# A four-layer decoder trunk on one core: joint key and value compression, a fixed first order, bias stores on ScalarE's queue, and a last sum by output halves

## The chip, the cores and the metric

The kernel runs on one core of one Trainium2 chip. The metric is the device time in microseconds (us) of one execution, and of several executions the median. TensorE (PE) multiplies matrices, VectorE (DVE) and ScalarE (ACT) work on elements, GpSimd (POOL) does little here, SyncE (SP) issues transfers (DMAs). Each engine takes its own instructions strictly in order.

## The reference

The input x has 256 rows of 1024 numbers. Four layers follow each other, each a feed-forward block, an attention and a second feed-forward block; all three normalise their input and their output:

```
x = x + 0.5 * rms_norm(swiglu(rms_norm(x, g[0]), ffn_w_in[i, 0], ffn_w_out[i, 0]), g[1])
hm = rms_norm(x, g[2])
m = sliding_sink_attention | nsa_attention | moba_attention   (layer i % 3)
x = x + rms_norm(m, g[3])
x = x + 0.5 * rms_norm(swiglu(rms_norm(x, g[4]), ffn_w_in[i, 1], ffn_w_out[i, 1]), g[5])
```

All attentions add a bias that depends on the distance of query and key, read from one table. Layer 1 (nsa_attention) also compresses keys and values: for each of the two, 15 overlapping blocks of 32 rows pass a two-layer perceptron:

```
flat = blocks.transpose(0, 1, 3, 2, 4).reshape(B, n_cmp, G, CMP_LEN * dh)
return jax.nn.gelu(flat @ w1) @ w2
```

## The kernel before, in words

The 256 rows are two chains (`Chain(0)`, `Chain(1)`) of 128 rows. Both use the same weights, which stream in once, as 625 pieces of 128x1024 f32 (512 KB, name `raw`, function `load`, four buffers). A piece is split (`feed`): ScalarE writes `hi`, its rounding to fp32r, and VectorE writes `lo`, the rest. x is transposed by TensorE (`split_T`, tile `trx`) and split likewise into `xh` and `xl`. A product is `hi·xh + lo·xh + hi·xl`: 12 matmuls of 512 columns for two pieces and one chain, in `proj` (into the tile `proj`) and in `accumulate` (into `acc`). Splits lie in a pool of 28 slots of 4 KB a partition (`k4`), which the attention stages share; `plan.want` keeps slots free for them.

Both chains are Python generators. A planner (`choose`) keeps a clock with estimated durations and takes, step by step, the chain that can go on earliest. TensorE's order is the order so written (`manual_schedule(engines=ORDERED)`); the order on the other engines, SyncE's DMAs among them, is set by a scheduler from the written order and its own estimates.

At the start, chain 0 transposes its x (x0), chain 1 its own (x1) some microseconds of the planner's clock later (`LATE`), and `first` squares x for the norm (`var`: two ScalarE squares into `junk`, two VectorE steps into `v`). `pres`, the norms' gains, is needed for `xh`.

`setup` starts after 30 steps. TensorE multiplies the table of biases with one-hot rows (tile `tab`), VectorE copies the rows, and four DMAs store them, each row repeated 32 times, in a scratch array in DRAM (`scratch<-k`, 384 KB each, 8 source partitions): table 1 in two halves of 8 heads, then table 0. They are issued by SyncE, in whose order all raws and bias loads stand, too. The attention of layer 0 reads table 1 back with shifted rows (`bias`, tile `bias`), four DMAs of 32 partitions for a group of heads.

In layer 1 `compress` runs first for keys (s = 0) and then for values (s = 1): 16 matmuls of 256 columns, written as 64x256, for each of four quarters of weights (`w1`, tile names `k<-w`) make the tile `hid` [64 partitions, 256]; a gelu of six instructions on 64 partitions, two transposes `hidT`, and the second layer `kcb` or `vcb` follow. (The hardware profile shows 32 matmul records for each of the two.) Beside it the attention's own steps run: `pv` products come in pairs whose results lie on the lower and upper 64 partitions.

At the end of each sublayer `accumulate` adds the last 12 products to the two halves (512 columns each) of `acc`, alternating between halves; `boundary` then squares both halves (`junk`), forms `r`, multiplies with the gain `g`, adds to x, and in the last layer sends x out.

Of the kernel before, what the change touches and what calls it, by code (L numbers as in the profile page):

```python
# [44 lines left out]
LATE = 6  # L45
SETUP = 30
SGAP = 8
# [5 lines left out]
ORDERED = {mybir.EngineType.PE}  # L53

# [196 lines left out]
class Engines:  # L251
    def __init__(self, nc, clock):
        self.tensor = TimedProducts(nc.tensor, clock)
        self.scalar = Timed(nc.scalar, "act", clock, 0.06, 0.00083)
        self.vector = Timed(nc.vector, "dve", clock, 0.065, 0.00105)
        self.gpsimd = Timed(nc.gpsimd, "pool", clock, 0.45, 0.001)
        self.sync = TimedLoads(nc.sync, clock)


@with_exitstack  # L260
def trunk(ctx: ExitStack, tc: tile.TileContext, x, rel, gains, pre, sinks, pos, w1, w2, wts, hot,
# [72 lines left out]
    def setup():  # L334
# [49 lines left out]
    def feed(urgent=False):  # L384

        load(plan.split + NRAW)
        if plan.split < len(halves) and (urgent or clock.now >= plan.at + PACE) and room() >= 2:
            i, half, n = halves[plan.split]
            r = raws.pop(plan.split)
            hi = p4.tile([P, HALF], F32R, tag="k4", name="hi")  # L390
            lo = p4.tile([P, HALF], F32R, tag="k4", name="lo")
            nc.scalar.activation(hi[:, :n], r[:, :n], AF.Copy)
            nc.vector.tensor_tensor(lo[:, :n], r[:, :n], hi[:, :n].bitcast(F32), op=ALU.subtract)
            parts.setdefault(i, []).append((hi, lo))
            ready_at[i] = max(when(lo) - 1.3 * half, ready_at.get(i, 0.0))
            plan.split += 1
            plan.at = max(plan.at + PACE, clock.now - 2.4)
            feed()
            return True
        return False  # L400

# [11 lines left out]
    class Chain:  # L413
# [36 lines left out]
        def split_T(self, src, q, norm=None):  # L450


            if q == 0:
                self.xh, self.xl = [], []
# [3 lines left out]
            ks = range(4 * q, 4 * q + 4)  # L458
            g = [None if norm is None else pres[:, norm, k:k + 1] for k in ks]
            for c, k in enumerate(ks):  # L460
                xh = px.tile([P, P], F32R, tag=f"xh{self.t}{k}", name="xh")
                if norm is None:
                    nc.scalar.activation(xh, p[:, c, :], AF.Copy)
                else:
                    nc.scalar.activation(xh, p[:, c, :], AF.Copy, scale=g[c])
                self.xh.append(xh)
            for c, k in enumerate(ks):
                xl = px.tile([P, P], F32R, tag=f"xl{self.t}{k}", name="xl")
                hi = self.xh[k].bitcast(F32)
                if norm is None:  # L470
                    nc.vector.tensor_tensor(xl, p[:, c, :], hi, op=ALU.subtract)
                else:
                    nc.vector.scalar_tensor_tensor(xl, p[:, c, :], g[c], hi, op0=ALU.mult,
                                                   op1=ALU.subtract)
                self.xl.append(xl)


        def first(self):
# [60 lines left out]
        def accumulate(self, acc, hh, hl, first, last):  # L539
# [4 lines left out]
            for n, (lhs, kk, part) in enumerate(terms):  # L544
                for nb in range(2):
                    nc.tensor.matmul(acc[nb], lhs[kk], got[kk][part][:, nb * 512:(nb + 1) * 512],
                                     start=first and n == 0, stop=last and n == 5)
# [340 lines left out]
        def attn_b(self, i):  # L888
# [22 lines left out]
            for s in range(2):  # L911
# [3 lines left out]
                if t == 0 and s == 0:  # L915
                    plan.want[3] = 3
# [29 lines left out]
    def compress():  # L946

        vbd = k4(2, [P, 2, 8, DH])
        nc.vector.memset(kcb, 0.0)
        hv = k2([P, 2, 2, 4, 32])  # L950
        for s in range(2):
# [4 lines left out]
            for e in range(2):  # L956
                rows = slice(DH * e, DH * e + DH)
                for m in range(2):
# [3 lines left out]
                        .broadcast_to([DH, 8, 4, NCMP]), op=ALU.add)  # L962
            drop(2)
            plan.want[2] -= 1
            ws = []
            for q in range(2):
                w = k4(3, [P, HALF])
                nc.sync.dma_start(w, w1[2 * s, :, q * HALF:(q + 1) * HALF])
                ws.append(w)
            p = bank([64, 2, P], "hid")  # L970
            for q in range(4):
                w = ws[q]
                yield when(w, xf), False
                for j in range(4 * q, 4 * q + 4):
                    at = (j % 4) * CMP_HIDDEN
                    nc.tensor.matmul(p.rearrange("p c n -> p (c n)"),
                                     xf[:, j].rearrange("p g n -> p (g n)"),
                                     w[:, at:at + CMP_HIDDEN], start=j == 0, stop=j == 15)
                drop(3)
                if q < 2:  # L980
                    w = k4(3, [P, HALF])
                    nc.sync.dma_start(w, w1[2 * s + 1, :, q * HALF:(q + 1) * HALF])
                    ws.append(w)
            drop(3)
            hid = k2([64, 2, P])
            q = k2([64, 2, P])
            nc.scalar.activation(q, p, AF.Square)
            nc.vector.tensor_scalar(q, q, 0.044715, 1.0, op0=ALU.mult, op1=ALU.add)
            nc.vector.tensor_tensor(q, q, p, op=ALU.mult)
            nc.scalar.activation(q, q, AF.Tanh, scale=GELU_C)  # L990
            nc.vector.tensor_scalar(q, q, 1.0, 0.5, op0=ALU.add, op1=ALU.mult)
            nc.vector.tensor_tensor(hid, q, p, op=ALU.mult)
            yield max(when(hid), free_bank()), False
            p = bank([P, 2, 64], "hidT")
            for c in range(2):
                nc.tensor.transpose(p[:, c, :], hid[:, c, :], ident[:64, :64])
            hid = k2([P, 2, 64])
# [112 lines left out]
```

## Time and profile before

| | us |
|---|---|
| median of three runs | 1984.88 |
| lowest, highest | 1984.06, 1987.67 |
| the profiled execution | 1989.9 |
| span of its instructions | 1988.1 |
| TensorE busy in it | 1947.6 |
| VectorE, ScalarE busy | 1236.2, 1040.7 |
| DMA, mean over the span | 179 GB/s |

The profiled execution is another execution than the three timed ones. Span is from its first instruction to its last; a little lies around it. Rows of the profile name the line of the helper that issues an operation (L228 a matmul, L235 a transpose, L210 a ScalarE or VectorE operation, L248 a DMA), so tiles, not lines, tell operations apart. A stretch's granted clock is TensorE's, 1.00 for 2.4 GHz throughout and 0.5 for 1.2 GHz throughout.

### The profile page before, as it was taken

How to read it: one execution, taken by the hardware profiler on the slowest of the kernel's cores; microseconds unless marked ns; L12 is line 12 of the kernel's file. 1: busy time of each engine (PE TensorE's matmuls, PEld its weight loads, DVE VectorE, ACT ScalarE, POOL GpSimd, SP SyncE). 2: the span in 40 equal slices, each digit the busy share in tenths (PEclk: the TensorE clock that was granted, in tenths of full speed). 3: DMA queues.
4: the chain of work that ended last, by engine and by line, in shares of the span. 5: the costliest groups of instructions: out<-in, count | busy, mean ns of one | idle time of the engine just before them, and what ended most of it. 6: DMA issues, size and time to landing. Idle time of an engine off the chain costs nothing. (4 is left out here: it accounts for less than half of the span.)

```text
span 1988.1 us, 27346 instructions
## 1 busy us (share of the span) xinstructions
PE 1947.6 (98%) x9948; PEld 1589.5 (80%) x9948; DVE 1236.2 (62%) x2271; ACT 1040.7 (52%) x1886; POOL 37.1 (2%) x62
## 2 busy tenths in 40 slices
PE   7999999999999999999999999999999999999998
PEld 6778878888888886788888887778888888878886
DVE  6556676556655648765566556466556655667553
ACT  6445665445544555554455446565445544665442
POOL 0000000000000000000000000000000000000000
PEclk9999999999999999999999999999999999999999
DMA  8578556555555454365555555556555555536551
GB/s 265 172 230 238 173 143 199 190 188 184 191 190 191 141 180 109 119 199 191 185 183 193 188 184 179 178 147 201 184 186 186 195 185 185 177 106 207 188 184 57
DMA packets 114099, 356.42 MB, mean 179 GB/s; under 512 B 12811, under 2 KB 30475, under 8 KB 113964
## 3 DMA queue, kind: packets, MB, share of 16 engines
q1 hardware_dynamic: 113964, 354.68, 55.3%
q8 instruction: 78, 1.28, 0.2%
q14 instruction: 57, 0.47, 0.1%
HBM read 352.01 MB, written 2.62 MB: 178 GB/s over the span
## 5 line engine op out<-in xcount | busy, mean ns | idle before, releaser
L210 DVE TENSOR_TENSOR lo<-raw,hi 128x1024 fp32r<-128x1024 f32 x625 | 761.0, 1223 | 378.0 <-ACT hi L210 346.9
L210 ACT ACTIVATE hi<-raw 128x1024 fp32r<-128x1024 f32 x625 | 660.6, 1064 | 383.4 <-PE acc L228 202.1
L228 PE MATMUL proj<-hi,xh 128*128 128x512 f32 (+1 forms) x1696 | 675.7, 400 | 2.6 <-DVE xl L210 1.9
L228 PE MATMUL proj<-lo,xh 128*128 128x512 f32 (+1 forms) x1696 | 658.7, 389 | 0.8 <-DVE lo L210 0.8
L228 PE MATMUL proj<-hi,xl 128*128 128x512 f32 (+1 forms) x1696 | 449.2, 387 | 0.0
L228 PEld LDWEIGHTS proj<-hi,xh 128*128 128x128 f32 x1696 | 320.6, 189 | 64.4 <-ACT xh L210 3.0
L228 PEld LDWEIGHTS proj<-lo,xh 128*128 128x128 f32 x1696 | 321.2, 189 | 61.5 <-DVE lo L210 1.1
L228 PEld LDWEIGHTS proj<-hi,xl 128*128 128x128 f32 x1696 | 316.2, 188 | 67.7
L228 PE MATMUL acc<-hi,hh 128*128 128x512 f32 x704 | 219.5, 393 | 3.0 <-ACT hh L210 3.0
L228 PE MATMUL acc<-lo,hh 128*128 128x512 f32 x704 | 217.7, 390 | 0.0
L228 PE MATMUL acc<-hi,hl 128*128 128x512 f32 x704 | 188.8, 390 | 0.0
L210 ACT ACTIVATE h<-proj,rh 128x256 f32<-128x256 f32 x176 | 82.0, 466 | 189.7 <-PE proj L228 189.6
L210 ACT ACTIVATE hh<-trh 128x256 fp32r<-128x256 f32 x176 | 66.9, 380 | 177.7 <-PE trh L235 177.6
L228 PEld LDWEIGHTS acc<-hi,hh 128*128 128x128 f32 x704 | 131.3, 189 | 30.1 <-ACT hh L210 3.7
L228 PEld LDWEIGHTS acc<-lo,hh 128*128 128x128 f32 x704 | 132.7, 189 | 27.9
L228 PEld LDWEIGHTS acc<-hi,hl 128*128 128x128 f32 x704 | 132.2, 188 | 27.7
L210 DVE SCALAR_TENSOR_TENSOR h<-h,proj 128x256 f32<-128x256 f32 x176 | 73.6, 418 | 120.0 <-ACT h L210 119.9
L210 DVE TENSOR_TENSOR hl<-trh,hh 128x256 fp32r<-128x256 f32 x176 | 73.9, 420 | 112.2 <-ACT hh L210 112.2
L210 ACT ACTIVATE k<-k,nm 128x128 f32<-128x128 f32 (+1 forms) x160 | 70.7, 446 | 35.8 <-DVE nm L210 35.7
L210 DVE SCALAR_TENSOR_TENSOR h<-proj,c,h 128x256 f32<-128x256 f32 x176 | 85.0, 483 | 5.2
L235 PE MATMUL trh<-ident,h 128*128 128x128 f32 x352 | 67.0, 272 | 0.0
L235 PEld LDWEIGHTS trh<-ident,h 128*128 128x128 f32 x352 | 48.7, 139 | 22.4 <-PE tab L228 0.6
(100 smaller groups left out, 1116.3 us busy)
## 6 DMA issues: line engine op xcount, KB each, us to landing
raw<-wts SPq DMA_DIRECT2D x624, 512.0 KB, 4.5
bias<-scratch SPq DMA_DIRECT2D x96, 128.0 KB, 5.0
g<-gains SPq DMA_DIRECT2D x12, 512.0 KB, 4.9
k<-w SPq DMA_DIRECT2D x8, 512.0 KB, 6.0
scratch<-k SPq DMA_DIRECT2D x4, 384.0 KB
out<-x SPq DMA_DIRECT2D x4, 256.0 KB, 2.1
x<-x SPq DMA_DIRECT2D x2, 256.0 KB
x<-x SPq DMA_DIRECT2D x1, 512.0 KB
```

Of the source, the lines that this page charges most:

```text
L210: return call(out, *args, **kw)
L228: self.engine.matmul(out, lhs, rhs, **kw)
L235: self.engine.transpose(out, src, ident)
```

## The change

Four things are changed.

- `compress` computes the hidden layer for keys and values together. The results of key branch and value branch lie on the lower and upper 64 partitions of one tile, written alternately; the sum over 16 positions is made in two parts of 8, each for its own four quarter loads; VectorE adds the parts. One gelu and one pair of transposes serve both. `plan.want[3]` keeps six slots instead of three.
- The start: `pres` is loaded first, by ScalarE's queue. Chain 0 alone begins. Its two transposed halves (`lift`) are followed by 16 transposes of the identity (`warm_up`); on ScalarE and VectorE the order of squares, splits of x and the first four splits of weights (`take`) is fixed. Chain 1 starts once chain 0 has taken its first weights, and its squares and splits come behind the third and fourth split.
- The four stores of the bias table are issued on ScalarE's queue.
- In the last `accumulate` of a sum, all six products of output half 0 come before the six of half 1.

```
+WARM = 16
-LATE = 6
+SPLITTERS = {mybir.EngineType.Activation, mybir.EngineType.DVE}
...
-                nc.sync.dma_start(scratch[i, h:h + 8],
-                                  rows[h:h + 8, i, :].unsqueeze(1).broadcast_to([8, REP, LT]))
+                nc.scalar_loads.dma_start(scratch[i, h:h + 8],
+                                          rows[h:h + 8, i, :].unsqueeze(1)
+                                          .broadcast_to([8, REP, LT]))
...
+    def warm_up():
+        p = bank([P, 4, P], "warm")
+        for n in range(WARM):
+            nc.tensor.transpose(p[:, n % 4, :], ident, ident)
...
             x_ = xt[self.t]
-            for q in range(2):
-                self.split_T(x_, q, 0)
-            self.v = self.var([x_[:, :512], x_[:, 512:]], 1.0)
+            if self.t == 0:
+                with tc.manual_schedule(engines=SPLITTERS):
+                    ps_ = [self.lift(x_, q) for q in range(2)]
+                    warm_up()
+                    self.v = self.var([x_[:, :512], x_[:, 512:]], 1.0)
+                    for q in range(2):
+                        self.split(ps_[q], range(4 * q, 4 * q + 4), 0)
+                        for _ in range(2):
+                            load(plan.split + NRAW)
+                            begun[:] = take()
+            else:
+                with tc.issue_after(begun[0].ins), tc.issue_after(begun[1].ins):
+                    for q in range(2):
+                        self.split_T(x_, q, 0)
+                    self.v = self.var([x_[:, :512], x_[:, 512:]], 1.0)
...
-            for n, (lhs, kk, part) in enumerate(terms):
-                for nb in range(2):
...
+            steps = [(n, nb) for n in range(6) for nb in range(2)]
+            if last:
+                steps.sort(key=lambda a: a[1])
+            for n, nb in steps:
...
-                    plan.want[3] = 3
+                    plan.want[3] = 6
...
+        sums = []
+        for m in range(2):
+            quarter(2 * m)
+            quarter(2 * m + 1)
+            yield max(when(*ws[4 * m:], *xfs), free_bank()), False
+            p = bank([P, 2, P], "hid")
+            for j in range(8):
+                at = (j % 4) * CMP_HIDDEN
+                for s in range(2):
+                    nc.tensor.matmul(p[HALVES[s]].rearrange("p c n -> p (c n)"),
+                                     xfs[s][:, 8 * m + j].rearrange("p g n -> p (g n)"),
+                                     ws[4 * m + j // 4 * 2 + s][:, at:at + CMP_HIDDEN], share=0.5,
+                                     start=j == 0, stop=j == 7)
+            drop(3, 4)
+            sums.append(k2([P, 2, P]))
+            if m:
+                nc.vector.tensor_tensor(sums[1], sums[0], p, op=ALU.add)
+            else:
+                nc.scalar.activation(sums[0], p, AF.Copy)
...
+        nc.scalar_loads.dma_start(pres, pre)
         for c in (slice(0, 512), slice(512, 1024)):
             nc.sync.dma_start(xt[0][:, c], x[:P, c])
-        nc.sync.dma_start(pres, pre)
         load(2)
         nc.sync.dma_start(xt[1], x[P:, :])
-        for t in range(2):
-            start(both[t].run(), t, t * LATE)
+        start(both[0].run(), 0)
         n = 0
         while running:
+            if both[0].at and not later:
+                later.append(True)
+                start(both[1].run(), 1)
```

SyncE's order around the stores, in the kernel before (`k_795` holds the bias rows; a wait on DMAHW is for an earlier transfer that counts on the same semaphore, and for a load from scratch also for the store it reads; DVE is VectorE):

```order
L248 DMA k_773<-hot 33x768 [waits DMAHW6_49,PE_49]
L248 DMA raw<-wts 128x1024 [waits DMAHW7_49,DMAHW2_49,DVE_49]
L248 DMA scratch<-k_795 256x1x384 [waits DVE_49] x2
L248 DMA raw<-wts 128x1024 [waits DMAHW3_49,DVE_49]
L248 DMA raw<-wts 128x1024 [waits DMAHW4_49,DVE_49]
...
L248 DMA scratch<-k_795 256x1x384 [waits DMAHW6_49]
```

and in the changed kernel at the same place:

```order
L249 DMA k_793<-hot 33x768 [waits PE_49]
L249 DMA raw<-wts 128x1024 [waits DMAHW2_49,DVE_49]
L249 DMA bias<-scratch 32x8x128 [waits DMAHW3_49,DMAHW1_49]
L249 DMA raw<-wts 128x1024 [waits DMAHW4_49,DVE_49]
L249 DMA bias<-scratch 32x8x128 [waits DMAHW5_49]
...
L249 DMA bias<-scratch 32x8x128 [waits DMAHW2_49,DMAHW0_49]
L249 DMA raw<-wts 128x1024 [waits DVE_49]
L249 DMA raw<-wts 128x1024 [waits DMAHW3_49,DVE_49]
L249 DMA bias<-scratch 32x8x128 [waits DMAHW4_49]
```

The stores have left SyncE's order, and the first three groups of bias loads, which stood dozens of raws later, now stand between single raws.

ScalarE's order at that place in the changed kernel:

```order
L211 ACTIVATE hi<-raw 128x1024 [waits DMAHW2_49,PE_49]
L249 DMA scratch<-k_815 256x1x384 [waits DVE_49] x2
L211 ACTIVATE hh<-trh 128x256 [waits PE_49,Activation_49]
L211 ACTIVATE h<-proj,rh 128x256 [waits PE_49]
L211 ACTIVATE hi<-raw 128x1024 [waits DMAHW6_49,DMAHW3_49]
L249 DMA scratch<-k_815 256x1x384
L211 ACTIVATE hi<-raw 128x1024 [waits DMAHW4_49]
...
L249 DMA scratch<-k_815 256x1x384 [waits DMAHW1_49]
L211 ACTIVATE hi<-raw 128x1024 [waits DMAHW7_49]
```

The third store follows a few ScalarE instructions later; the fourth waits for an earlier store's completion, with splits behind it.

TensorE's order at the start, in the kernel before (x_95 is x0, x_96 is x1):

```order
L235 MATMUL trx<-ident,x_95 128x128 x8
L235 MATMUL trx<-ident,x_96 128x128 x8
L228 MATMUL proj<-hi,xh 128x512
L228 MATMUL proj<-lo,xh 128x512
...
```

and in the changed kernel:

```order
L236 MATMUL trx<-ident,x_95 128x128 x8
L236 MATMUL warm<-ident 128x128 x16
L229 MATMUL proj<-hi,xh 128x512
L229 MATMUL proj<-lo,xh 128x512
...
L229 MATMUL proj<-hi,xl 128x512 x4
L236 MATMUL trx<-ident,x_96 128x128 x8
```

The transposes of x1 have moved behind the first twelve products, and fillers stand in their place.

## Rows read from the trace of the kernel before

**Rows 1.** From the page: busy us of each engine, share of the span, instructions.

```profile
PE 1947.6 (98%) x9948; PEld 1589.5 (80%) x9948; DVE 1236.2 (62%) x2271; ACT 1040.7 (52%) x1886; POOL 37.1 (2%) x62
```

**Rows 2.** What TensorE waited for, whole span, longest first: instruction, releaser, us in total, times, longest.

```profile
PE trx L235 <- DMA x<-x: 8.9, 2, 5.3
PE trx L235 <- DVE x L210: 6.4, 11, 2.0
...
PE hid L228 <- PE trp L235: 0.9, 1, 0.9
...
PE hid L228 <- DMA k<-w: 0.7, 1, 0.7
```

**Rows 3.** Timeline from the start to 55 us, all engines: start us, us, engine, line, operation, out<-in, count, and in brackets the idle time before and what ended it.

```profile
3.59 1.94 PE L235 MATMUL trx<-ident,x 128*128 128x128 f32 x8 [3.59 <-DMA x<-x]
7.93 1.06 ACT L210 ACTIVATE hi<-raw 128x1024 fp32r<-128x1024 f32 x1 [2.79 <-DMA raw<-wts]
9.02 1.23 DVE L210 TENSOR_TENSOR lo<-raw,hi 128x1024 fp32r<-128x1024 f32 x1 [3.69 <-ACT hi L210]
10.87 1.97 PE L235 MATMUL trx<-ident,x 128*128 128x128 f32 x8 [5.34 <-DMA x<-x]
13.06 0.77 PE L228 MATMUL proj<-hi,xh 128*128 128x512 f32 x1 [0.23 <-DVE xl L210]
...
14.05 0.63 PE L228 MATMUL proj<-hi,xh 128*128 128x512 f32 x1
14.48 0.63 PE L228 MATMUL proj<-lo,xh 128*128 128x512 f32 x1
...
49.45 1.06 ACT L210 ACTIVATE hi<-raw 128x1024 fp32r<-128x1024 f32 x1 [1.27 <-DMA raw<-wts]
...
50.83 0.79 PE L228 MATMUL acc<-hi,hh 128*128 128x512 f32 x1 [2.57 <-ACT hh L210]
...
55.01 1.06 ACT L210 ACTIVATE hi<-raw 128x1024 fp32r<-128x1024 f32 x1 [0.47 <-DMA raw<-wts]
```

**Rows 4.** Stretches of the span (from:to in us): their length, busy us and instructions of each engine in the order PE, PEld, DVE, ACT, POOL, then the granted clock, the DMA engines' busy share, GB/s.

```profile
3.00:13.00 10.00, 3.91 (x16) 3.04 (x16) 4.11 (x11) 5.94 (x15) 0.55 (x1) 1.00 0.93 314
...
50.00:54.00 4.00, 3.17 (x8) 2.55 (x9) 2.29 (x3) 2.61 (x5) 0.00 (x0) 0.57 0.87 293
86.00:91.00 5.00, 5.00 (x24) 4.14 (x23) 3.60 (x5) 2.37 (x3) 0.00 (x0) 1.00 0.45 54
681.80:685.30 3.50, 3.48 (x9) 2.81 (x9) 2.79 (x13) 3.50 (x11) 0.35 (x1) 0.51 0.52 177
735.00:805.00 70.00, 64.89 (x694) 47.99 (x693) 58.46 (x262) 41.95 (x153) 5.10 (x7) 1.00 0.42 117
```

**Rows 5.** SyncE's issues of the bias table's stores and the first loads from it, timeline as in rows 3 (the us are those of issuing).

```profile
84.59 1.50 SPq L248 DMA_DIRECT2D scratch<-k  x2
...
101.11 0.69 SPq L248 DMA_DIRECT2D scratch<-k  x1
...
119.55 0.69 SPq L248 DMA_DIRECT2D scratch<-k  x1
...
148.12 0.92 SPq L248 DMA_DIRECT2D bias<-scratch  x2
```

**Rows 6.** Transfers from 84 to 112 us: GB/s in 40 slices of 0.7 us; the raws issued there, KB each and median us to landing; and, from the page, the same of all raws.

```profile
GB/s 53 0 11 53 48 53 72 50 50 48 132 220 171 50 51 48 72 205 224 74 50 50 46 181 195 290 269 392 310 222 211 205 195 127 87 236 191 54 50 46
...
raw<-wts SPq DMA_DIRECT2D x7, 512.0 KB, 12.4
...
raw<-wts SPq DMA_DIRECT2D x624, 512.0 KB, 4.5
```

**Rows 7.** TensorE's timeline behind the stores, columns as in rows 3.

```profile
106.09 0.50 PE L228 MATMUL proj<-hi,xh 128*128 128x512 f32 x1 [0.60 <-ACT hi L210]
107.35 0.50 PE L228 MATMUL proj<-lo,xh 128*128 128x512 f32 x1 [0.76 <-DVE lo L210]
```

**Rows 8.** Timeline rows of layer 1, columns as in rows 3: transposes ahead of the stretch of rows 4 at 681.8; hid products and pv pairs; the first gelu.

```profile
677.24 1.03 PE L235 MATMUL trq<-ident,k 128*128 128x128 f32 x8
...
745.87 3.67 PE L228 MATMUL hid<-k,k 128*64 128x256 f32 x16
...
749.58 0.38 ACT L210 ACTIVATE k<-hid 64x256 f32<-64x256 f32 x1 [1.49 <-PE hid L228]
750.29 0.28 DVE L210 TENSOR_SCALAR k<-k 64x256 f32<-64x256 f32 x1
750.60 0.41 DVE L210 TENSOR_TENSOR k<-k,hid 64x256 f32<-64x256 f32 x1
751.24 0.40 ACT L210 ACTIVATE k<-k 64x256 f32<-64x256 f32 x1
...
773.18 1.15 PE L228 MATMUL pv<-k,pT 128*64 128x64 f32 x32
```

**Rows 9.** The end, columns as in rows 3: twelve products of one chain between the first row and the second, and ScalarE's two squares behind the last product.

```profile
1974.93 0.62 PE L228 MATMUL acc<-hi,hh 128*128 128x512 f32 x2
...
1977.65 0.38 PE L235 MATMUL trh<-ident,h 128*128 128x128 f32 x2
...
1981.39 0.60 ACT L210 ACTIVATE junk<-acc 128x512 bf16<-128x512 f32 x1 [2.94 <-PE acc L228]
...
1982.11 0.60 ACT L210 ACTIVATE junk<-acc 128x512 bf16<-128x512 f32 x1
```

More of the change, by code (lines that the diff above doesn't have):

```diff
@@ L387, in feed @@
         if plan.split < len(halves) and (urgent or clock.now >= plan.at + PACE) and room() >= 2:
[L388 to L397, printed above, removed]
+            take()
             feed()
@@ L400, in feed, with take @@
         return False
+    def take():
+        i, half, n = halves[plan.split]
+        r = raws.pop(plan.split)
+        hi = p4.tile([P, HALF], F32R, tag="k4", name="hi")
+        lo = p4.tile([P, HALF], F32R, tag="k4", name="lo")
+        made = [nc.scalar.activation(hi[:, :n], r[:, :n], AF.Copy),
+                nc.vector.tensor_tensor(lo[:, :n], r[:, :n], hi[:, :n].bitcast(F32),
+                                        op=ALU.subtract)]
+        parts.setdefault(i, []).append((hi, lo))
+        ready_at[i] = max(when(lo) - 1.3 * half, ready_at.get(i, 0.0))
+        plan.split += 1
+        plan.at = max(plan.at + PACE, clock.now - 2.4)
+        return made
+    def warm_up():
+        p = bank([P, 4, P], "warm")
+        for n in range(WARM):
+            nc.tensor.transpose(p[:, n % 4, :], ident, ident)
     gains_on = {}
@@ L971, in compress @@
[L971 to L993, printed above, removed]
@@ new lines, in compress @@
+        drop(3, 2)
+        hid, q = sums
+        nc.scalar.activation(hid, q, AF.Square)
+        nc.vector.tensor_scalar(hid, hid, 0.044715, 1.0, op0=ALU.mult, op1=ALU.add)
+        nc.vector.tensor_tensor(hid, hid, q, op=ALU.mult)
+        nc.scalar.activation(hid, hid, AF.Tanh, scale=GELU_C)
+        nc.vector.tensor_scalar(hid, hid, 1.0, 0.5, op0=ALU.add, op1=ALU.mult)
+        nc.vector.tensor_tensor(hid, hid, q, op=ALU.mult)
+        yield max(when(hid), free_bank()), False
+        p = bank([P, 2, P], "hidT")
@@ new lines, in compress @@
+        for c in range(2):
+            nc.tensor.transpose(p[:, c, :], hid[:, c, :], ident)
+        hid = k2([P, 2, 64])
+        nc.vector.tensor_copy(hid, p[:, :, :64])
+        for c in range(2):
+            nc.vector.tensor_copy(
+                hv[:, c], p[:, c, 64:].rearrange("p (g n) -> p g n", n=32).unsqueeze(2)
+                .broadcast_to([P, 2, 4, 32]))
+        yield max(when(hid), free_bank()), False
+        p = bank([P, 64], "kcb")
+        for c in range(2):
+            nc.tensor.matmul(p, w2s[:, 0, c].rearrange("p a d -> p (a d)"), hid[:, c, :],
+                             start=c == 0, stop=c == 1)
@@ new lines, in compress @@
+        for e in range(2):
+            rows = slice(DH * e, DH * e + DH)
+            nc.vector.tensor_copy(
+                kcb[rows, :, e, :],
+                p[rows, :].rearrange("p (g e n) -> p g e n", e=2, n=16)[:, :, e, :])
+        for G in range(2):
+            yield max(when(hv), free_bank()), False
+            p = bank([P, DH], "vcb")
+            for c in range(2):
+                nc.tensor.matmul(p, hv[:, c, G].rearrange("p a n -> p (a n)"),
+                                 w2s[:, 1, c, 0, :], start=c == 0, stop=c == 1)
+            nc.vector.tensor_tensor(vbd[:, G], p.unsqueeze(1).broadcast_to([P, 8, DH]),
+                                    bm.unsqueeze(2).broadcast_to([P, 8, DH]), op=ALU.mult)
```

69 lines of the change are left out of this document (24 added, 45 removed).

## The prediction

> **What bounds the kernel now.** I read the busy shares first. TensorE is busy 1947.6 of 1988.1 us, 98% [rows 1], so a part of the change is worth what it takes out of those 1947.6 us, out of the 40.5 us in which TensorE stands, or out of what follows its last matmul. Next the list of TensorE's waits, the longest first: no cause has more than 8.9 us [rows 2]. So this is a kernel whose time is a sum of small places, and each part of the change has its own place.
>
> The start, in the timeline: x0 is transposed at 3.59 and the first product runs at 13.06, after the second chain's x1 has landed and been transposed at 10.87 [rows 3]. The first eight products start 0.43 us apart, later ones 0.23 apart (twelve in 1977.65 − 1974.93 = 2.72) [rows 3, 9]. Until 55 us ScalarE's splits wait for raws [rows 3]: the weights' arrival, not TensorE, sets the pace there.
>
> The bias table, in SyncE's issues: two stores are issued at 84.59, raws right behind them, another store at 101.11 and one at 119.55 [rows 5]. Through 86 to 91 the DMA engines are 45% busy and move 54 GB/s [rows 4]; the row in 0.7 us slices shows 50 GB/s whenever a store is alone [rows 6]. A store of 384 KB (393 kB) thus takes 393/50 = 7.9 us; two, one behind the other, end near 101. Raws caught behind them took 12.4 us to land (median of that stretch), 4.5 otherwise [rows 6]. TensorE then stood 0.60 for a hi and 0.76 for a lo [rows 7].
>
> The compression, 735 to 805: TensorE is busy 64.9 of 70 us and VectorE 58.5 [rows 4], so both nearly bound it. The end: behind the last product ScalarE squares the two halves of acc one after the other, at 1981.39 and 1982.11 [rows 9]; v, r, x and the output's transfer follow.
>
> **The change, part by part.**
>
> *Start.* The new order has TensorE do the eight x0 transposes, 16 fillers, and then products; x1's transposes come behind the first twelve products. Fillers cost 1.94/8 = 0.243 us each at the rate of row 3.59, 3.9 in all, so they end at 3.59 + 1.94 + 3.9 = 9.4. The first hi ends at 7.93 + 1.06 = 8.99 and its lo, begun at 9.02, at 10.25 [rows 3]. So products start near 9.5 instead of 13.06: 3.6 earlier. Of that, x1's transposes (1.97) still have to be done, now inside the stream: 1.6 is left. Raws 2 and on arrive no sooner, since the engines were already 93% busy from 3 to 13 us [rows 4], and splits wait for them until 55. But at 50.83 TensorE lost 2.57 us waiting for an hh queued behind a hi that waited for its raw, and after it ran at granted clock 0.57 [rows 3, 4], that is mostly at 1.2 GHz, which cost about half of the 3.17 us busy in that window, 1.4. If the new interleaving avoids that, 4 more come off. Bounds −1 and −5.5; I take **−2.5**, nearer to the first, because the raws set the pace in that stretch.
>
> *Fillers and the clock.* The row bearing on it is 681.8 to 685.3: behind eight transposes at 677.24, 24 products of 48 columns and eight more transposes, the granted clock is 0.51, about 1.2 GHz [rows 4, 8]. So transposes needn't leave the clock high. If the fillers don't raise it, the first eight products keep their 0.43 pitch, 8 × 0.20 = 1.6 us. Since raws are late in any case, this moves the sum by 0 to 1.6, inside the bounds above. The Trainium skill (TensorE: Matmul & The Clock Gate, Part 4: PE-mode transpose) says that the full clock does not engage for transposes, which don't count as busy in the same way; by that rule the start is worth −0.9 instead of −2.5.
>
> *Stores on ScalarE's queue.* Removed from SyncE: four issues (1.50 + 0.69 + 0.69 = 2.9 us of its queue, unused time) and the blocking of the raws behind the stores, worth the 1.36 us that TensorE stood. Added: the four issues on ScalarE, 2.9 us of a queue that has room there. But what the order shows behind it weighs more. SyncE now meets the first bias load between two raws, and that load waits for the second store; the next bias group waits for the third, the group behind it for the fourth. In the kernel before, the first bias load was issued at 148 [rows 5], when all stores were long done. So three times SyncE holds raws until a store has landed. Walked on the times of before: products first miss their half (the 36th) at 106.09 − 0.60 = 105.5 [rows 7]. A pair of halves lasts two chains × 12 products, 5.4 us, so the next three halves are due near 110.3, 111.2 and 115.7. Store 2 lands near 101.5; the 36th raw is issued at 102.5, lands at 107 (4.5), and its hi and lo take 1.06 + 1.23 [rows 3]: 109.3, 3.8 late. Store 3 lands near 109.5, raws 37 and 38 land near 115, split 117.3: due at 111.2 + 3.8, so another 2.7. Store 4 cannot be issued before store 2 is done (ScalarE waits for it, with a hi and an hh behind it that are not due yet); it lands near 117.3, the 39th raw near 122.8, split at 125: another 2.6. Together 9.1, less the 1.36: +8. That is the lower bound of this walk. With raws landing as late as 12.4, the last of them is split at 133 instead of 125, +16; stores that share engines with raws, and 1.4 for products at half clock after each long wait, make the upper bound +19. The lowest bound is that nothing waits: −1.4. I take **+12**, in the middle of 8 and 16: raws 37 to 39 run beside one store, not behind two.
>
> The Trainium skill (DMA: Bandwidth & Descriptors, Issuing engines are not separate DMA queues) says that transfers issued by several engines run on the same 16 DMA engines and interleave, and that a second issuer saves only the issuing time. By that rule the stores take their 7.9 us each on either queue, and raws still share with them; the sum would keep the 1.36 and come out at +13. No run of before has a second queue.
>
> *Compression.* Before: 64 hid products, 16 of them in 3.67 us, the pitch (3.67 − 0.38)/15 = 0.219, together 14.0 us. After: the same 64, alternately for the two branches, into the lower and the upper 64 partitions of the output. The nearest rows with such pairs are pv: 32 products of 64 columns in 1.15, 0.030 each, so 0.120 for 256 columns, 7.7 us in all [rows 8]. That is −6.3 where pairs overlap likewise, 0 where they don't. One chain of gelu goes (VectorE 0.28 + 0.41 and a like pair behind the tanh, ScalarE 0.38 + 0.40) [rows 8], and with it an hidT; an add and a copy come. TensorE's hid waits of 0.9 and 0.7 [rows 2] can go. Against it: VectorE is 84% busy, so part of TensorE's gain may turn into waits; all cores and projections of this layer are reordered. Bounds −10 and +3; I take **−5.5**, near the pv row.
>
> *Last sum.* Half 0 of acc is complete six products (6 × 0.23 = 1.4 us) earlier, so its square and product with g run beside the rest. ScalarE's pitch between the two squares, 1982.11 − 1981.39 = 0.72, goes [rows 9]; nothing else shortens, since v needs the second. Bounds 0 and −1; **−0.7**. hl is needed after four products instead of eight; it is one VectorE instruction behind an hh that the first product waits for anyway, and four products take 0.9, so I count no stall.
>
> *Inner boundaries.* The same sum order at each of the other sublayers lets x be ready up to 0.7 earlier for its own chain; the other chain's products cover most of it. TensorE's waits for x are 6.4 in eleven places [rows 2]. Bounds 0 and −5; **−1**.
>
> Sum: −2.5 + 12 − 5.5 − 0.7 − 1 = +2.3 against the profiled execution's 1989.9, 1992.2. The median of the three runs is 1984.88, 5.0 lower, so the forecast is **1987** us, no change: about 4 us (0.2%) is what a measurement of this kernel can tell.
>
> **Rivals.**
>
> *A: the held raws cost nothing (faster).* If the stores, alone on their queue, end by about 97 instead of 101.5, or the splits run far enough ahead, raws come in time, and the 1.36 goes too. For it: through 86 to 91 the engines were 55% idle [rows 4]. Against: nothing in the change makes a store's pieces larger. The sum is 2.3 − 13.4 = −11.1: 1974.
>
> *B: the stall is larger (slower).* Place: SyncE's queue between 84 and 130. Raws, bias loads and stores share engines, each store takes 11 instead of 7.9 us, and the 36th to 39th raws are late by some 20 in all. It decides from the point where store 2 lands after about 104. The price is +8 on the forecast: 1995. For it: raws' 12.4 beside stores [rows 6]. Against: only one raw is in flight while SyncE waits.
>
> *C: paired hid products don't overlap (slower).* Each keeps its 0.219; VectorE gives no gain either. +5.5: 1992.5. For it: each is 256 columns of f32, longer than any paired row here; against: pv does overlap.
>
> *D: fillers and boundaries do nothing.* +2 to +3: 1989.5, still no measurable change.
>
> **The numbers.** Forecast and D together 0.41, of which 0.33 lie within 4 us and 0.08 are shared between the sides; A 0.25, B 0.20, C 0.14. Faster: A and 0.04, 0.29; within 0.2%: 0.33; slower: B, C and 0.04, 0.38. The forecast's own range is 1981 to 1991. To hold 8 in 10 it reaches to A and to B and not beyond their middles: 1974 to 1998.
>
> **What would show it.** First product near 9.5 and the second chain's transposes behind it; products at 0.43 or 0.23 from there tell whether fillers raised the clock. In SyncE's issues, a bias load that stands until a store has landed, raws behind it, and products waiting for hi or lo of raws, 9 to 17 us between 100 and 130: if those waits sum to under 2, A holds; over 17, B. Hid starts 0.11 to 0.13 apart show pairs, 0.22 shows C. At the end, the two squares must no longer stand back to back after the last product. The forecast is wrong if the whole is outside 1981 to 1991, and the bias-table stretch is the step to look at first.

## The result

The changed kernel is slower: median 2003.02 us (five runs, 1997.13 to 2007.01) against 1986.33 us, a ratio of 1.0082, 95% interval 1.0068 to 1.0096, or +16.3 us by that ratio. That is outside the prediction's range, 1981 to 1991. The profiled execution has a span of 2002.1 us, 14.0 more than that of before; it is split up below.

### The profile page after: what moved, and what is told of

It is laid out like the page before. It is cut to its first block, busy times and chain, and to the rows that moved or that the text cites. A ratio compares the mean times of both kernels' runs of the same rounds, so it can differ in the third digit from the quotient of the medians.

```text
span 2002.1 us, 27385 instructions
## 1 busy us (share of the span) xinstructions
PE 1949.1 (97%) x9962; PEld 1595.2 (80%) x9962; DVE 1235.4 (62%) x2267; ACT 1040.8 (52%) x1885; POOL 43.1 (2%) x62
## 3 DMA queue, kind: packets, MB, share of 16 engines
q10 hardware_dynamic: 1200, 1.67, 0.7%
## 4 chain that ended last, share of the span: by engine, by line
PE 88%; DMA 4%; ACT 3%; DVE 3%; issue 1%; SPq 0%; POOL 0%; ACTq 0%; DVEq 0%; POOLq 0%
PE proj L229 54%; PE acc L229 28%; ACT k L211 2%; PE trh L236 2%; DMA bias<-scratch 2%; DVE k L211 1%; DMA raw<-wts 1%; PE trx L236 1%; DMA scratch<-k 1%; PE pv L229 1%; DVE lo L211 1%; PE trp L236 1%; ACT hi L211 1%; DVE pT L211 0%; PE trq L236 0%
## 5 line engine op out<-in xcount | busy, mean ns | idle before, releaser
L229 PE MATMUL proj<-hi,xh 128*128 128x512 f32 (+1 forms) x1696 | 672.9, 398 | 17.9 <-ACT hi L211 14.6
L229 PE MATMUL acc<-hi,hh 128*128 128x512 f32 x704 | 224.9, 393 | 2.6 <-ACT hh L211 2.6
L229 PE MATMUL acc<-lo,hh 128*128 128x512 f32 x704 | 223.2, 391 | 0.0
L211 POOL TENSOR_TENSOR r<-v,mhalf 128x1 f32<-128x1 f32 x48 | 36.0, 750 | 1843.0 <-DVE v L211 1843.0
```

The source lines that it names most:

```text
L211: return call(out, *args, **kw)
L229: self.engine.matmul(out, lhs, rhs, **kw)
```

## The profile after

TensorE's waits in the whole span: instruction, releaser, us in total, times, longest.

```profile
PE proj L229 <- ACT hi L211: 14.6, 1, 14.6
PE acc L229 <- DVE mx L211: 5.4, 8, 1.7
PE trx L236 <- DMA x<-x: 3.9, 1, 3.9
PE proj L229 <- DVE lo L211: 3.0, 6, 0.7
...
PE trx L236 <- DVE x L211: 2.6, 3, 2.0
```

One wait of 14.6 us for one hi stands first; before, the whole list held nothing like it [rows 2]. The waits for x at the boundaries have gone from 6.4 in eleven places to 2.6 in three.

To see where the rest went I took marks from both traces. The two kernels run the same 7584 weight products (matmuls of proj and acc with hi or lo), and between 200 and 600 in the same order, so the start of the n-th of them is the same amount of work done in either. Lengths in us between marks, and for the last column from the last product's start to the span's end:

```
kernel            to 200th  200-600  600-2600  2600-3000  3000-6600  6600-6800  6800-7584  end
before              65.1      97.1     500.0      174.9      882.5       76.3      185.2    7.0
changed             62.8     117.8     499.9      166.4      880.5       83.0      185.2    6.5
```

The stretches are, in that order: the start; the bias table's stores; the rest of layer 0 and layer 1's first feed-forward; layer 1's attention with its compression; layers 1 to 3 up to the last attention; layer 3's attention; the last feed-forward; the end. The differences, −2.3, +20.7, −0.1, −8.5, −2.0, +6.7, 0 and −0.5, add up to the 14.0. Two stretches lose, and only one of them was in the prediction.

**The bias table.** SyncE's and ScalarE's issues there (start, us, queue), ScalarE's splits and TensorE's long wait, from three timelines of after:

```profile
78.83 0.35 SPq L249 DMA_DIRECT2D raw<-wts  x1
99.95 0.34 SPq L249 DMA_DIRECT2D bias<-scratch  x1
100.39 4.41 SPq L249 DMA_DIRECT2D raw<-wts  x1
104.86 9.89 SPq L249 DMA_DIRECT2D bias<-scratch  x4
114.79 0.92 SPq L249 DMA_DIRECT2D raw<-wts  x2
...
82.34 1.99 ACTq L249 DMA_DIRECT2D scratch<-k  x2
85.62 3.35 ACTq L249 DMA_DIRECT2D scratch<-k  x1
99.96 0.69 ACTq L249 DMA_DIRECT2D scratch<-k  x1
100.69 1.06 ACT L211 ACTIVATE hi<-raw 128x1024 fp32r<-128x1024 f32 x1 [6.27 <-DMA scratch<-k]
117.50 1.06 ACT L211 ACTIVATE hi<-raw 128x1024 fp32r<-128x1024 f32 x1 [15.48 <-DMA raw<-wts]
...
103.06 0.50 PE L229 MATMUL proj<-lo,xh 128*128 128x512 f32 x1 [0.51 <-DVE lo L211]
118.61 0.80 PE L229 MATMUL proj<-hi,xh 128*128 128x512 f32 x1 [14.58 <-ACT hi L211]
```

SyncE issues nothing between 79.2 and 99.95: the bias load waits for the second store, as foreseen, and the store lands when foreseen (two of 393 kB at 50 GB/s). But the one raw let out behind it at 100.39 is not split until 117.50, 17.1 us later, where 4.5 was taken. Its issue alone takes 4.41 us instead of 0.35, and then half of it does not move. ScalarE, too, stood 6.27 us, since the fourth store in its order waited for the second to land; TensorE still had products and lost only 0.51 to that, at 103.06. The transfers' packets show what held the raw (q1 is SyncE's queue, q10 ScalarE's; packets, MB, share of 16 engines' time), here for 100 to 104, 104 to 108, 108 to 112 and 112 to 116; a raw is 128 packets of 4096 bytes, a bias load 256 of 512:

```profile
q10 hardware_dynamic: 130, 0.20, 43.5%
q1 hardware_dynamic: 136, 0.07, 6.3%
...
q10 hardware_dynamic: 131, 0.19, 39.6%
q1 hardware_dynamic: 208, 0.33, 24.8%
...
q10 hardware_dynamic: 130, 0.20, 44.0%
q1 hardware_dynamic: 136, 0.07, 6.2%
...
q1 hardware_dynamic: 614, 0.53, 41.7%
q10 hardware_dynamic: 95, 0.13, 24.7%
```

In the first three windows the stores take 40 to 44% of all engine time, about that of seven engines in sixteen, at 50 GB/s (0.20 MB in 4 us). The other engines do little, since SyncE's issues stand. Of the raw's 128 packets 64 pass near 106, the other 64 only from 112 on, as the fourth store ends. The first bias load is split likewise: one half passes from 101 on, the other near 107, between the third store and the fourth. So on the engines that carry stores, a load in the other queue waits for a whole store, and then the next store goes ahead of the load behind it. By the Trainium skill (DMA: Bandwidth & Descriptors, Queues, rings and completion order) an engine drains a whole packet of descriptors from one ring before it takes another. The rows here agree in kind: what changes turns is a transfer's share of an engine, not a row of it.

TensorE then runs at 1.2 GHz: products from 118.61 to 124, and again from 134 to 138. Two windows of after around the wait (length; busy us and count of PE, PEld, DVE, ACT, POOL; granted clock; DMA share; GB/s):

```profile
107.00:124.00 17.00, 4.93 (x11) 3.55 (x12) 1.77 (x2) 2.48 (x3) 0.00 (x0) 0.50 0.80 159
...
134.00:138.00 4.00, 3.72 (x9) 2.94 (x10) 3.93 (x6) 2.59 (x4) 0.00 (x0) 0.57 0.87 252
```

Between the marks 200 and 600 TensorE's waits grow from 1.4 us to 17.7. The other 4.4 of the 20.7 us are products at 1.2 GHz.

**Layer 3's attention**, from mark 6600 to mark 6800: the first row is before, the second after.

```profile
1719.60:1795.90 76.30, 73.91 (x556) 58.70 (x555) 53.44 (x188) 51.47 (x155) 2.19 (x4) 1.00 0.39 120
```

```profile
1727.40:1810.40 83.00, 79.39 (x556) 64.08 (x555) 55.08 (x190) 52.26 (x154) 2.19 (x4) 0.92 0.39 117
```

TensorE does as many instructions as before, but is busy 5.5 us longer at a granted clock of 0.92; its waits grow only from 2.4 us to 3.6. So most of the 6.7 us is clock. In its order more products now come ahead of the attention cores (73 instead of 61 before the first one), which then run with fewer products between them; their small matmuls wait for VectorE (2.7 us for mx, 0.7 before), and the clock falls.

**The gains** are there. Hid products, and the end:

```profile
753.28 3.67 PE L229 MATMUL hid<-k,k 128*64 128x256 f32 x32
766.05 3.67 PE L229 MATMUL hid<-k,k 128*64 128x256 f32 x32
...
1994.76 0.60 ACT L211 ACTIVATE junk<-acc 128x512 bf16<-128x512 f32 x1 [1.81 <-PE acc L229]
1996.12 0.60 ACT L211 ACTIVATE junk<-acc 128x512 bf16<-128x512 f32 x1 [0.67 <-PE acc L229]
```

32 hid products take what 16 took [rows 8]; the trace has their starts 0.007 and 0.21 us apart in turn, so each pair runs together. The first square runs beside the last products; the second starts 0.72 behind the first in [rows 9] and here as soon as its half of acc is done.

## Experiments

All ratios are to the kernel before on the same chip, with 95% intervals. The lengths between marks, one profiled execution each:

```
kernel            to 200th  200-600  600-2600  2600-3000  3000-6600  6600-6800  6800-7584
only_store          62.6     115.7     500.3      174.1      882.5       76.2      186.3
no_store            63.7      97.1     499.3      167.8      880.4       79.0      185.2
late_bias           61.9     104.2     502.1      168.6      880.4       79.9      185.2
store16             63.2     102.6     500.5      168.4      881.3       81.3      185.3
table0_later        62.4      99.0     498.3      166.0      880.8       79.8      185.3
only_acc            67.0      97.1     500.3      173.6      881.0       81.4      185.3
acc_but3            63.0     117.7     500.3      165.7      881.0       77.3      185.2
only_compress       62.9      97.1     501.7      169.8      883.8       76.3      185.2
only_start          63.5      97.0     500.1      172.2      883.1       76.2      185.3
no_store_no_warm    63.0      97.1     501.0      166.1      881.0       83.0      185.2
best_sp             63.1      97.0     500.6      164.0      880.9       75.8      185.2
best_sp16           63.8      97.3     500.4      165.4      881.4       75.8      185.3
```

### The stores' queue, alone and undone

only_store, from the kernel before; no_store is the reverse edit of the changed kernel:

```
-                nc.sync.dma_start(scratch[i, h:h + 8], ...
+                nc.scalar_loads.dma_start(scratch[i, h:h + 8], ...
```

> The kernel before with the stores' issue on ScalarE's queue and nothing else. In the order the first bias load then stands behind 35 raws, as in the changed kernel, instead of 58. Theory (the hoisted bias loads hold SyncE until stores have landed): the whole loss of that stretch comes back, 20 us by the two traces, so a ratio near 1.010, with one TensorE wait for a hi of 12 to 16 us behind the table. Rival (the loss needs the earlier start or the joint compression as well): within 4 us of before.

Measured: 2005.08 us, ratio 1.009 (1.0075 to 1.0104). SyncE again stands until the second store has landed, and TensorE's wait is 12.89 us:

```profile
101.23 0.34 SPq L248 DMA_DIRECT2D bias<-scratch  x1
101.67 4.20 SPq L248 DMA_DIRECT2D raw<-wts  x1
105.92 9.04 SPq L248 DMA_DIRECT2D bias<-scratch  x4
...
118.19 0.80 PE L228 MATMUL proj<-hi,xh 128*128 128x512 f32 x1 [12.89 <-ACT hi L210]
```

> The changed kernel with the four stores back on SyncE's queue; the first bias load then stands behind 58 raws. Theory: the 20 us go, 2003 becomes 1982 to 1984, ratio about 0.998, with 6 to 7 us still lost in layer 3's attention. Rival (the second queue is not the cause, the early start meets the stores at a worse moment): 1995 or more.

Measured: 1980.16 us, ratio 0.9961 (0.9946 to 0.9975). The stretch is back at 97.1 us; the time is better than expected, as layer 3 takes 79.0 us in this profile and not 83.0. So this part alone brings the loss and needs no other part for it; the rival falls. It also turns the sign of the whole change.

### What of it: the bias loads' place, the number of engines, the later stores

late_bias, in the changed kernel (`latest` collects the issues of raws):

```
+                with tc.issue_after(latest[-24].ins):
                     nc.sync.dma_start(b[q:q + REP], src)
```

> The changed kernel, with the bias loads kept behind later raws in SyncE's order (the first one behind 64 raws instead of 35); the stores stay on ScalarE's queue, on eight engines. Theory (the place of the bias loads is the cause, not the second queue): no wait over 4 us near the table, 1979 to 1985, ratio about 0.997. Rival (the stores on a second queue starve raws on the shared engines whatever SyncE does): a stall of 8 us or more stays, 1990 or more.

Measured: 1991.34 us, ratio 1.0019 (1.0006 to 1.0031), which is 0.6% above no_store. With no bias load in SyncE's way the stretch falls from 117.8 to 104.2, but not to 97.1. A wait of 4.38 us stays, for an hh behind a hi whose raw is late:

```profile
115.86 1.06 ACT L211 ACTIVATE hi<-raw 128x1024 fp32r<-128x1024 f32 x1 [5.51 <-DMA raw<-wts]
...
118.59 1.22 PE L229 MATMUL acc<-hi,hh 128*128 128x512 f32 x2 [4.38 <-ACT hh L211]
```

By the stretch my theory was two thirds right: 13.6 us go with the bias loads' place, and 7.1 stay. The time lies in the rival's range, 1990 or more, though the wait is half of the rival's 8 us. The 7.1 us come with raws that meet stores on the engines. Whether the queue makes them is not shown: the four raws issued from 87 to 97 land 13.1 to 13.4 us after their issue, and no_store's four from 85 to 99 take 10.8 to 16.2. But ScalarE issues all four stores within 11.6 us here (81.40 to 93.01), and SyncE's order in no_store spreads them over 35.1 (83.22 to 118.28).

store16, in the changed kernel:

```
-            for h in range(0, H, 8):
-                nc.scalar_loads.dma_start(scratch[i, h:h + 8], ...
+            nc.scalar_loads.dma_start(scratch[i],
+                                      rows[:, i, :].unsqueeze(1).broadcast_to([H, REP, LT]))
```

> The changed kernel, with each table's two stores of 8 heads made one of 16 heads (786 KB, 16 source partitions), still on ScalarE's queue; the first bias load still stands behind 35 raws and waits for the first table's store. Theory (what hurt is how long a store lies on eight DMA engines and what queues behind it there; a store from 16 partitions uses 16): the store moves at about 100 GB/s, lands 8 us after its issue, before the held raw is due, and the stall falls from 14.6 to under 3 us; time as with the stores on SyncE, 1979 to 1983, ratio 0.996 to 0.998. Rival (a store's rate is not bound by the number of engines, or holding SyncE at all costs the time): 15 us of wait remain, ratio 1.006 or more.

Measured: 1986.9 us, ratio 1.0001 (0.9988 to 1.0013). The rate was right; GB/s from 78 to 125 us in 40 slices show 94 to 105 while the stores run, twice the 50 of [rows 6]:

```profile
GB/s 96 126 261 150 17 94 99 98 101 95 105 95 98 101 101 95 101 97 59 0 199 230 171 268 380 425 230 310 199 227 206 242 255 255 214 334 277 230 226 380
...
82.70 1.33 ACTq L249 DMA_DIRECT2D scratch<-k  x2
...
100.78 2.36 DVE L211 TENSOR_TENSOR lo<-raw,hi 128x1024 fp32r<-128x1024 f32 x2 [11.07 <-DMA scratch<-k]
...
102.06 1.22 PE L229 MATMUL acc<-lo,hh 128*128 128x512 f32 x2 [3.72 <-DVE lo L211]
```

The landing was wrong: both tables' stores go out together at 82.70, so the first bias load passes only at 100.61, not near 91. But no store is left then, the three raws behind it land 5.0 to 7.2 us after their issue, and TensorE does not wait for them. Its longest wait, 3.72 us instead of 14.58, is for something else: VectorE stood 11.07 us with a lo until a store had landed, presumably because the stored rows lay in the slot that this lo takes, which no run tests. SyncE's hold is as long as in the changed kernel, and the stretch loses 5.5 us instead of 20.7. So the hold alone does not make the 14.6. The time lies between the theory's and the rival's.

table0_later, in the changed kernel (`hews` collects the hi splits):

```
-                nc.scalar_loads.dma_start(scratch[i, h:h + 8], ...
-                yield clock.now + SGAP, False
+                with tc.issue_after(hews[-1].ins):
+                    nc.scalar_loads.dma_start(scratch[i, h:h + 8], ...
+                yield clock.now + (SGAP if (i, h) != (1, 8) else 40), False
```

> The changed kernel, with table 0's two stores (the third and the fourth) held on ScalarE's queue until some ten pieces later; the first bias load still stands early, behind 36 raws, and waits for table 1's stores, and bias loads still stand between raws. Theory (the 14.6 us are a held raw that then meets the third and fourth store on their eight DMA engines, transfer by transfer): raws issued behind the first bias load land within 8 us instead of 17, the longest wait falls to 3 to 6 us, time 1986 to 1993, ratio 1.000 to 1.003. Rival (the hold of SyncE alone makes the stall): the longest wait stays at 10 us or more, ratio 1.006 or more.

Measured: 1984.49 us, ratio 0.9975 (0.9961 to 0.9989). Better than expected: the longest waits of TensorE in the stretch are 1.64 and 1.67, and its length is 99.0.

```profile
82.57 1.27 ACTq L249 DMA_DIRECT2D scratch<-k  x1
89.65 0.68 ACTq L249 DMA_DIRECT2D scratch<-k  x1
...
132.95 0.68 ACTq L249 DMA_DIRECT2D scratch<-k  x1
139.57 0.67 ACTq L249 DMA_DIRECT2D scratch<-k  x1
...
92.27 0.34 SPq L249 DMA_DIRECT2D bias<-scratch  x1
92.70 6.59 SPq L249 DMA_DIRECT2D raw<-wts  x3
```

The edit did more than I had meant: the second store, too, is issued later, at 89.65, and the first bias load passes at 92.27, before that store can have landed at 50 GB/s. SyncE thus stands 7.3 us instead of 20.8. The raw let out at 92.70 meets the second store alone and lands 9.7 us after its issue, a little more than the 8 expected. So the rival, the hold alone, is not tested here; store16 speaks against it. How much each of the two moves gives is not separated. The run shows that a second queue and early bias loads need not cost more than 1.9 us, with the stores spread over 57 us; what costs is a held raw that meets a row of stores.

### The order of the last sum

only_acc makes that part alone, from the kernel before; acc_but3 takes it back, in the changed kernel, for one sum:

```
-            self.accumulate(acc, hh, hl, False, True)
+            self.accumulate(acc, hh, hl, False, True, (i, f) != (3, 0))
...
-            if last:
+            if last and halves_first:
                 steps.sort(key=lambda a: a[1])
```

> The kernel before with the last sum's products ordered by output half and nothing else. TensorE's order in layer 3's attention then is that of the changed kernel, with more products ahead of the cores. Theory (this part alone brings the loss in layer 3): +6.7 there, -3 at the inner boundaries, -0.5 at the end, so +3, ratio 1.0015, and about 14 us at half clock in layer 3. Rival (layer 3's loss comes from another part): -3.5, ratio 0.998.

Measured: 1986.47 us, ratio 0.9993 (0.9982 to 1.0005): no change, where I expected +3 and the rival said −3.5; the interval leaves out both. In its profile, the slowest of twelve executions (1993.95 us), layer 3 takes 81.4 us instead of 76.3, at a granted clock of 0.91:

```profile
1727.00:1787.00 60.00, 56.23 (x449) 44.85 (x448) 36.79 (x145) 37.31 (x120) 0.55 (x1) 0.91 0.38 108
```

The loss in layer 3 thus comes from this part, but it differs from execution to execution: over the seven profiles with the new order there, which is the same in all seven, it is 79.0 to 83.0, over the seven others 75.8 to 77.3. The gains elsewhere pay for it: from 600 to 2600 nothing, but from 3000 to 6600 all ten profiles with the new sums have 880.4 to 881.4, the four others 882.5 to 883.8.

> The changed kernel, with the products in the sum ahead of layer 3's attention (first feed-forward of layer 3) alternating between halves as before, and all other sums by output half. TensorE's order in layer 3's attention is then that of the kernel before. Theory (the order there flips through that one sum): 2 to 7 us less than the changed kernel, 1996 to 2001, and no half clock between 1730 and 1790. Rival (layer 3's loss has nothing to do with the order): within 1.5 us of the changed kernel in that stretch.

Measured: 1998.33 us, ratio 1.0057 (1.004 to 1.0074), that is 5 us under the changed kernel by the ratios, whose intervals overlap a little. Layer 3 takes 77.3, at clock 0.97:

```profile
1728.00:1788.00 60.00, 58.54 (x393) 45.73 (x393) 42.29 (x165) 42.27 (x136) 2.19 (x4) 0.97 0.41 127
```

Twelve products in another order, ahead of that stage, turn the planner's choices behind them. My "no half clock" there is not borne out fully.

### Compression and start alone

only_compress takes `compress` and `plan.want[3] = 6` of the changed kernel; only_start the new start.

> The kernel before with the joint compression (and its six kept slots) and nothing else. Theory (pairs of hid products overlap and TensorE takes most of it): 32 hid products in 3.7 us, and -7 to -9 us, ratio 0.996. Rival (the gain of layer 1 in the changed kernel comes from the other order of sums): -2 to -4.

Measured: 1982.09 us, ratio 0.9972 (0.996 to 0.9984), −5.6 us, between the theory's −7 to −9 and the rival's −2 to −4. Hid products are as in the changed kernel, 32 in 3.67 us. Layer 1's attention gains 5.1 us in this profile, not 8.5; only_acc gains 1.3 there. The rest lies within what executions differ: only_start, with the old order in this stretch, has 172.2 instead of 174.9.

> The kernel before with the new start (pres on ScalarE's queue, fixed order of the first splits, 16 fillers, chain 1 later) and nothing else. Theory (raws set the pace until 55 us, so an earlier first product is worth little by 65 us): first product near 8.5, but 0 to -2 us at the 200th product against runs with the old start, ratio 0.999 to 1.0005. Rival (the start keeps most of its 4.6 us): ratio 0.9975 or less.

Measured: 1987.4 us, ratio 1.0003 (0.9994 to 1.0013). The first product starts at 8.8 instead of 13.1; at the 200th product 63.5 against 65.1. But only_store and only_compress, with the old start, are there at 62.6 and 62.9, and only_acc at 67.0. So the 2.3 us of the table above are mostly the one execution of before, with its wait at 50.83 [rows 3]. All ten profiles with the new start lie between 61.9 and 63.8, so about 1 us may be the change's; the time shows none.

no_store_no_warm: no_store with `WARM = 0`.

> The changed kernel with stores on SyncE's queue (the run no_store) and without the 16 fillers. Theory (raws set the pace at the start, fillers change no time): the first products start 0.43 us apart if fillers had raised the clock, but the 200th product and the whole lie within 2 us of no_store, ratio 0.995 to 0.997. Rival (fillers save the half-clock products): 1.5 to 3 us longer than no_store at the 200th product.

Measured: 1982.37 us, ratio 0.9964 (0.9952 to 0.9976). The third and fourth product of no_store_no_warm, and then of no_store, with fillers:

```profile
10.18 0.63 PE L229 MATMUL proj<-hi,xh 128*128 128x512 f32 x1
10.61 0.63 PE L229 MATMUL proj<-lo,xh 128*128 128x512 f32 x1
```

```profile
9.95 0.40 PE L229 MATMUL proj<-hi,xh 128*128 128x512 f32 x1
10.18 0.40 PE L229 MATMUL proj<-lo,xh 128*128 128x512 f32 x1
```

Fillers do raise the clock: 0.23 between products instead of 0.43. It changes no time, since at the 200th product the two are 0.7 us apart, the one without fillers ahead.

### Without the parts that cost

best_sp is acc_but3 with the stores on SyncE's queue; best_sp16 makes of each table's two stores one of 16 partitions.

> The changed kernel with both harmful parts taken back: stores on SyncE's queue, and the sum ahead of layer 3's attention alternating as before. Theory: no_store's gain of 8 us and 2 to 5 of layer 3: 1974 to 1979, ratio 0.9935 to 0.996. Rival (the two don't add): as no_store, ratio 0.9961.

Measured: 1976.25 us, ratio 0.9935 (0.992 to 0.9949), 12.4 us under its runs of before and faster than both kernels.

> As best_sp, with each table stored by one DMA from 16 partitions, both issued by SyncE behind the 35th raw. Theory (a store moves at 98 GB/s on 16 engines, 16 us for both tables in all, and they now stand together ahead of the next raws): raws behind them are late by as much as behind the two eight-engine stores, the wait there is 1 to 4 us, the bias loads stand late; within 3 us of best_sp. Rival (the shorter store frees the queue sooner): 1.4 us or more faster.

Measured: 1977.05 us, ratio 0.9941 (0.9924 to 0.9958). No difference to best_sp can be told; the stretch takes 97.3 and 97.0. The longest wait there is 0.9 us, less than the 1 to 4 expected.

## Why the prediction was wrong

| step | predicted | in the profile | |
|---|---|---|---|
| start | −2.5 | −2.3 | by chance: timed alone it is 0 |
| stores | +12 | +20.7 | the hold right, the held raw's landing wrong |
| compression | −5.5 | −8.5 with layer 1's other differences; −5.6 timed alone | right |
| last sum at the end | −0.7 | −0.5 | right |
| inner boundaries | −1 | −2.1 | right in sign |
| layer 3's order | 0 | +6.7 | not counted |

The step that failed is "I take **+12**, in the middle of 8 and 16: raws 37 to 39 run beside one store, not behind two", with its walk of 4.5 to 12.4 us for a landing. The hold of SyncE was read rightly from the order, up to the store whose landing ends it, and the store landed as walked. But the raw let out then ran behind two stores, the third and the fourth, and its issue and landing took 17.1 us. I took a second queue as milder. It was not, and the trace of before had the price: 12.4 is the median of seven raws [rows 6], and the longest of them took 16.2, behind two stores in the same queue:

```profile
DMA to landing us min/median/max: 8.1/12.4/16.2
```

Before, that raw was issued early enough for TensorE to wait little; in the changed kernel the raw was let out only when its products were nearly due. Put in order, a raw landed 5.0 to 7.2 us after its issue with no store ahead (store16), 9.7 with one (table0_later), and 16.2 or 17.1 with two.

The waits from 100 to 130 sum to 15.6 us, within the 9 to 17 that the prediction named as its sign, but 14.6 of them are one raw and not three holds of some 3 us each. With the 2.1 us at 134 and the products at 1.2 GHz they make the 20.7, less the 1.4 of waits that were there before. (The walk's own due times give 2.3 and 3.2 for its second and third raw instead of 2.7 and 2.6, 9.3 in place of 9.1; this changes nothing.) Rival B named the place, the shared engines and a price of 20, but not the mechanism: stores kept their 50 GB/s, and its condition, store 2 later than 104, did not come about; it landed at 99.9.

The second step is an omission. I priced the last sum's new order at the end and the boundaries, and gave no term to what it does to the planner. The order of layer 3's attention on TensorE could have been read beforehand: it is moved by that one sum. That the clock can fall inside a layer, behind a stretch of small matmuls, was in the trace of before, at 681.8 [rows 4, 8], but I used the row for fillers alone. Against the profiled execution +2.3 was forecast and +14.0 measured: the stores make 8.7 of the difference and layer 3 makes 6.7, while compression and inner boundaries take back 3.0 and 1.1.

Fillers: I let rows 4 and 8 speak for "transposes needn't leave the clock high", and cited the Trainium skill (TensorE: Matmul & The Clock Gate, Part 4: PE-mode transpose) beside it. Here the measurement decides against the rule: with the sixteen fillers behind the eight transposes of x0, and no product ahead of them, the next products ran 0.23 us apart, the pitch of 2.4 GHz, and 0.43 apart without the fillers.

Open: what of table0_later's gain belongs to the second store's later issue, what of late_bias's 7.1 us to the queue and what to the stores' closeness, what SyncE's hold costs by itself, and why the half-clock windows in layers 1 and 3 differ between executions of one kernel.

## What to carry to other kernels

When a store moves to another queue, look at where the scheduler puts the loads that read it: a load that waits for a slow store holds every transfer behind it on its queue. Do not price a transfer beside a slow store as slowed; price it as waiting for whole stores, by the longest landing in the trace and not the median, and let nothing urgent be issued while several are queued. Ask of any reordering, however small, what a planner behind it makes of it, by reading the order of the next stages.

## What the runs showed of the hardware

- Stores from 8 partitions move 50 GB/s, from 16 partitions 94 to 105 [rows 6, and store16].
- A 512 KB load lands 5.0 to 7.2 us after its issue with no such store ahead, 9.7 behind one and 16.2 or 17.1 behind two, the 16.2 in the stores' own queue (before) and the 17.1 in the other (changed).
- A DMA's issue can itself stand: 4.41 us on SyncE and 3.35 on ScalarE while stores are queued, 0.34 and 0.69 otherwise. In the kernel before, too, the four raws issued from 87.27 on took 13.79 us to issue.
- Pairs of f32 products of 256 columns into the two halves of the output's partitions overlap fully: 3.67 us for 32, as for 16 unpaired.
- Executions of one kernel differ by several us, and the slower ones have the lower granted clock: of only_acc's twelve the fastest took 1981.27 us at 0.998 and the slowest 1993.95 at 0.992. One profile's difference of 2 to 3 us in a stretch is no evidence.
